# Hymba-style layer on one core: the order of the last norm, weight sums held back before the first keys, and weight sums made during the attention scores

## The chip, the cores and the metric

The kernel runs on one core of one Trainium2 chip. The metric is the device time of one execution in microseconds (us), the median of three runs. The core's engines are TensorE (PE in the profile, with PEld for its weight loads), VectorE (DVE), ScalarE (ACT), GpSimd (POOL) and SyncE (SP); each works off its own queue of instructions in the order in which they were written. Transfers are issued from SyncE's queue, and a few from ScalarE's.

## The reference

One layer over 512 tokens of width 2048, all in float32:

```python
def reference(x, mem, ...):
    h = x
    xn = _rmsnorm(h, norm_mix[l])
    y = xn @ w_in[l]
    o_gdn = _gdn_group(y[..., :GDN_COLS], ...)      # gated DeltaNet, 8 heads x 128
    o_rwkv = _rwkv_group(y[..., GDN_COLS:], ...)    # RWKV-7, 16 heads x 64
    h = h + jnp.concatenate([o_gdn, o_rwkv], axis=-1) @ w_out[l]
    h = h + _cross_attention(_rmsnorm(h, norm_xattn[l]), _rmsnorm(mem, norm_mem[l]),
                             wq, wk, wv, wo)        # 4 heads of 512, 256 memory tokens
    hn = _rmsnorm(h, norm_mlp[l])
    h = h + jnp.square(jax.nn.relu(hn @ mlp_w_up[l])) @ mlp_w_down[l]   # hidden 8192
    return _rmsnorm(h, norm_final)
```

`_rmsnorm(x, g)` is `x * rsqrt(mean(x*x) + 1e-6) * g`.

## The kernel before, in words

**Products.** Every float32 operand of a large product is cut into two float32r halves: ScalarE casts the high half (`whi`), VectorE subtracts it from the raw value for the low half (`wlo`), and TensorE adds hi·hi, hi·lo and lo·hi. A weight tile is 128x1024 (512 KB), loaded by SyncE into one of a few raw buffers (`wraw`, `w`, `ws`); each tile of halves has three buffers in the attention stages.

**Stages**, by the trace's time: the input projection (`py`, 0 to 907 us) with the chains of the two recurrent groups woven in; the keys of the memory tokens (`kp`, weights `in_wk`; the memory itself is loaded as `in_memT` into `wraw` and `mraw` and cut into `mhl`), from 907; the product of keys and query weights (`kq`), from 1025; values (`vp`, `vo`), from 1118; the output projection (`op`), from 1295; the scores (`sc`), 1456 to 1546; attention times values (`at`), to 1640; the MLP up (to 2280) and down (to 2874), which use Strassen's products; and the final norm with the outputs, to 2890.

**What sets the order.** In the scores and some other stages the program's text is the order, apart from the transfers, which a scheduler places by their buffers. In most other stages a planner does it: chains of Python generators yield instructions or conditions (`after(...)`, a lambda on `events`), and `run()` issues next the instruction with the earliest estimated start, plus 150 ns times the chain's rank for engines other than TensorE. All its instructions carry the line of the helper that records them, L257.

**Weight sums.** Strassen's products of the MLP down need the sums s1 to s4 of the quarters A11, A21, A22, A12 of the weight `w_dm`. For 13 pairs (e, m) of 2048 columns they are made ahead: `presum` loads a piece of the four quarters (tiles `ds`, or later `ab`, `sl`, `acc`, `h`), VectorE makes the four sums in place, and SyncE stores them to DRAM (`sd_s`), to be loaded later like a weight. `presums` does so in the projection and key stages in pieces of 410 columns with one set of `ds` buffers (40 pieces, 32 of 410 and 8 of 408 columns); `remaining` and `leftover` make the rest in the MLP.

**First keys.** In the recurrent part, `ndri`, `sr` and `bg16T`, `bg16U` are small transfers that carry a triangular inverse between engines: VectorE's `GA` and `GB` are written to `ndri`, then copied to `sr`, worked on by GpSimd, and written out as `bg16T` and `bg16U`. They stand on SyncE's queue in a row with the loads of the second `in_memT` tile, of the `in_wk` tiles and of `mraw`.

**Scores.** Two heads at a time (`g`), eight iterations each. An iteration loads a tile of 128x1024 in two halves (`kqr`, from DRAM `kqd`; three buffers), cuts it (`kqh`, `kql`), and runs 24 matmuls.

**The last norm.** When the MLP's last product for a token group t (128 tokens, t = 0 to 3) and column group g (512 columns) is added, `final` squares the tile on ScalarE with a running sum, and multiplies it by the gain for g = 0 and 1; when all four of a t are done, `store` forms the row's factor (reduce, square root, reciprocal), scales the four tiles (g = 0, 1 on ScalarE, g = 2, 3 on VectorE together with the gain) and writes each out (256 KB). T4 is the last of the last unit's products; t = 2, 3 finish first, then 0 and 1.

Of the kernel before, what the change touches and what calls it, by code (L numbers as in the profile page):

```python
# [17 lines left out]
P = 128  # L18
# [55 lines left out]
def build(tc, I, out):  # L74
# [53 lines left out]
    def split(src, hi, lo, gain=None):  # L128
        if gain is None:
            S.copy(hi, src)  # L130
            V.tensor_tensor(out=lo, in0=src, in1=hi.bitcast(F32), op=ALU.subtract)  # L131
        else:
            S.activation(hi, src, AF.Copy, scale=gain)
            V.scalar_tensor_tensor(out=lo, in0=src, scalar=gain, in1=hi.bitcast(F32),
                                   op0=ALU.mult, op1=ALU.subtract)
# [264 lines left out]
    def presum(e, m, c, n, d, LD=Lane(nc.sync, "SP", margin=5000.0), ST=SY):  # L400
        tt = lambda o, a, b, op=ALU.subtract: DV.tensor_tensor(out=o, in0=a, in1=b, op=op)
        src = I["w_dm"][e, m]
        a11, a21, a22, a12 = b = [x[:, 0:n - c] for x in d]
        for i in (A21, A22, A11, A12):
            yield LD.dma_start(b[i], src[i][:, c:n])
        for j, op in (("s1", tt(a22, a21, a22, ALU.add)), ("s3", tt(a21, a11, a21)),
                      ("s2", tt(a11, a22, a11)), ("s4", tt(a12, a12, a11))):
            yield op
            yield ST.dma_start(Sd[e, m, j][:, c:n], op[5])
            upto[e, m, j] = upto.get((e, m, j), 0) + n - c  # L410

    def presums(d, width, stop):
        while todo and not stop():
            e, m = todo.pop(0)
            for c in range(0, 2048, width):
                if c and stop():
                    todo.insert(0, (e, m))
                    return
                yield from presum(e, m, c, min(c + width, 2048), d, Lane(nc.sync, "SP", margin=5000.0), Lane(nc.sync, "SP", 0.0, 0.0))

    hk = [("w", I["wk"][n][:, h * 1024:(h + 1) * 1024]) for n, h in kpo]
# [1261 lines left out]
    def turned():  # L1683
        g, _, probs = turn.pop(0)
        for e in range(2):
            for mt in range(2):
# [4 lines left out]
                S.copy(phi[kk], pt)  # L1691
                V.tensor_tensor(out=plo[kk], in0=pt, in1=phi[kk].bitcast(F32), op=ALU.subtract)

    for g in range(2):
        banks = (("mm", 2), ("mg", 2), ("mg", 2), ("mm", 2)), (("scr", 1), ("scg", 1), ("mx", 2), ("mx", 2))
        pts = [psb(f"sc{g}_{t}", *banks[g][t]) for t in range(4)]
        for n2 in range(8):
            cnt[0] += 1
            raw = pw.tile([P, 1024], F32, tag="wraw", name=f"kqr{cnt[0]}", bufs=NWR)
            for i in range(2):  # L1700
                nc.sync.dma_start(raw[:, i * 512:(i + 1) * 512], KQd[2 * n2 + i][:, g * 512:(g + 1) * 512])
            wh = pw.tile([P, 1024], F32R, tag="whi", name=f"kqh{cnt[0]}", bufs=NWS)
            wl = pw.tile([P, 1024], F32R, tag="wlo", name=f"kql{cnt[0]}", bufs=NWS)
            split(raw, wh, wl)
            if g == 0 and n2 < 6:
                second(2 * n2 + 4)
                second(2 * n2 + 5)
            its = [(i, t) for i in range(2) for t in range(4)] if n2 < 7 else [(i, t) for t in range(4) for i in range(2)]
            for i, t in its:
                n = 2 * n2 + i  # L1710
                w1, w2 = wh[:, i * 512:(i + 1) * 512], wl[:, i * 512:(i + 1) * 512]
                a1, a2 = hh_[n][:, t * P:(t + 1) * P], hl_[n][:, t * P:(t + 1) * P]
                mm(pts[t], a1, w1, start=(n == 0), stop=False)
                mm(pts[t], a1, w2, start=False, stop=False)
                mm(pts[t], a2, w1, start=False, stop=(n == 15))
            if g == 0 and n2 == 6:
                norm()
            if g == 1 and n2 < 2:
                softmax(2 * n2)
                softmax(2 * n2 + 1)  # L1720
            if g == 1 and n2 == 3:
                turned()
        if g == 1:
            for n in range(2):
                begun.append((psb(f"at{n}", "mg"), *wload(VOd[0][:, :, n * P:(n + 1) * P])))
                attend(*begun[n], 0)
        turn.append((g, pts, []))
        if g == 1:
            for t in range(4):
                softmax(t)  # L1730
# [202 lines left out]
    def splits():  # L1933
        for u in units:
            if u[0] == "d" and u[1:3] in INSITU and u[1:] not in PRE:
                for i, w in order_of(u):
                    for x in xs(u):
                        yield (after("sum", u, w, x) if isinstance(w, str) else after("raw", u, w, x))
                        r = raws[u, {"s2": A11, "s3": A21, "s4": A11 if u == units[-1] else A12}.get(w, w), x]
                        halves[u, i, x] = hl = yield from take(hfree)  # L1940
                        yield from cut(r, *hl)
                        events.add(("half", u, i, x))
                        if w not in (A11, "s2") and (w != A12 or u == units[-1]):
                            wfree.append(r)
                continue
            if u[0] == "d":
                for i, w in order_of(u):
                    for x in xs(u):
                        yield after("raw", u, i, x)
                        halves[u, i, x] = hl = yield from take(hfree)  # L1950
                        yield from cut(raws[u, i, x], *hl)
                        wfree.append(raws[u, i, x])
                        events.add(("half", u, i, x))
                continue
            for i, w in order_of(u):
                yield ready((u, w))
                halves[u, i] = hl = yield from take(hfree)
                yield from cut(sums[u, w] if isinstance(w, str) else raws[u, w], *hl)
                events.add(("cut", u, w))
                events.add(("half", u, i))  # L1960
                if w in ("s1", "s2"):
                    release(u, w, sfree)
                elif w == "s3":
                    release(u, A21)
                elif w == "s4":
                    wfree.append(raws[u, A12])
                elif w != A12:
                    release(u, w)
# [204 lines left out]
    def downout(u, t, tag):  # L2173
        e, g = u[1:3]
        yield after("H", 3, 3)

        def add(m, half, src):
            h = H[2 * half + t, 2 * g + m]
            return tt(h, h, src)

        (x, kx) = banks_of[u, tag, t]
        mul = lambda i: after("mul", u, i, t)
        outs = {B11: (tag, 0, 0, 0), B21: ("mm", 0, 0, 1), T2: (tag, 0, 1, 0), T1: ("mg", 1, 1, 0),
                T3: (tag, 1, 1, 0), B22: ("mg", 0, 1, 1), T4: (tag, 1, 0, 1)}
        for i, _ in order_of(u):
            tg, m, half, end = outs[i]
            yield mul(i)
            b, kb = banks_of[u, tg, t]
            yield add(m, half, b)
            events.add(("snap", u, i, t))  # L2190
            if end:
                events.add(kb)
            if e == 3 and u[3:] != (0,) and i in (B21, T3, B22, T4):
                chain(final(2 * half + t, 2 * g + m), 0 if g and i == T4 else 2 if g == 0 else 1)
# [77 lines left out]
    def final(t, g):  # L2272
        h = H[t, g]
        c = yield from take(cfree)
        yield AC.activation(c, h, AF.Square, accum_out=cols5[t][:, g:g + 1])
        cfree.append(c)
        if g not in (2, 3):
            yield after("wf")
            yield tt(h, h, wf[g], ALU.mult)
        got[t] += 1  # L2280
        if got[t] == 4:
            chain(store(t), 1 if t > 1 else 0.2)

    def store(t):
        a, b = rows5[t][:, 0:1], rows5[t][:, 1:2]
        yield DV.tensor_reduce(out=a, in_=cols5[t], axis=AX.X, op=ALU.add)
        yield AC.activation(b, a, AF.Sqrt, scale=1.0 / 2048)
        yield DV.reciprocal(out=b, in_=b)
        yield after("wf")
        for g in (0, 1, 2, 3):  # L2290
            h = H[t, g]
            if g in (2, 3):
                yield DV.scalar_tensor_tensor(out=h, in0=h, scalar=b, in1=wf[g], op0=ALU.mult, op1=ALU.mult)
            else:
                yield AC.activation(h, h, AF.Copy, scale=b)
            yield (SV if g < 2 else SY).dma_start(out[t * P:t * P + P, g * 512:g * 512 + 512], h)

    def phase():
        return sum(("mul", v, B11, 0) in events for v in units[32:])
# [166 lines left out]
```

## Time and profile before

| | us |
|---|---|
| runs | 2887.84, 2888.71, 2888.92 |
| median of the runs | 2888.71 |
| the profiled execution, span from first to last instruction | 2890.0 |
| TensorE busy | 2862.2 (99%) |
| VectorE, ScalarE, GpSimd busy | 2333.9, 1571.7, 214.7 |
| moved by the DMA engines | 553 MB, 191 GB/s in the mean |

The profiled execution's span, 2890.0 us, is its own time; it stands 1.3 us above the median of the runs. The granted clock of TensorE was 0.999 of full speed in the mean. A duration read below is one of that execution. In rows of the trace the first number is the start in us from the span's begin, the second the duration; brackets give the engine's idle time ahead of the instruction and what ended it.

### The profile page before, as it was taken

To read this page: it belongs to the slowest core of one execution; us is meant where nothing else is said; L and a number is where in the kernel's file an instruction comes from. 1 tells how busy PE (TensorE), PEld (TensorE's weight loads), DVE (VectorE), ACT (ScalarE), POOL (GpSimd) and SP (SyncE) were. 2 spreads that over 40 slices of the span, in tenths; PEclk is the share of its full clock that TensorE was granted. 3 is DMA by queue.
4 is the path that set the end of the run, shared out by engine and by line. 5 is a ranking of instruction groups with operands and counts; after the bars stand their busy time and mean duration, and the time that the engine had idled before them with its cause. 6 is when DMAs were issued, how large, how long until landed. Compare 5 with 4: busy or idle time off the path is not lost.

```text
span 2890.0 us, 49168 instructions
## 1 busy us (share of the span) xinstructions
PE 2862.2 (99%) x18794; PEld 2419.1 (84%) x18794; DVE 2333.9 (81%) x3559; ACT 1571.7 (54%) x2233; POOL 214.7 (7%) x539
## 2 busy tenths in 40 slices
PE   9999999999999999999999999999999999999998
PEld 7877887877877888889988888888888888888887
DVE  7787787787877877769956898899998878786888
ACT  6555555645656655664445556555555644454544
POOL 0213213213212100000000000000000000000000
PEclk9999999999999999999999999999999999999999
DMA  5656656657656788784422354666565878887733
GB/s 191 166 147 176 176 149 187 165 154 189 180 161 200 214 257 274 232 292 151 124 95 88 110 164 153 199 195 207 189 200 178 292 249 277 295 257 247 265 101 110
DMA packets 321212, 553.01 MB, mean 191 GB/s; under 512 B 101128, under 2 KB 188428, under 8 KB 320976
## 3 DMA queue, kind: packets, MB, share of 16 engines
q1 hardware_dynamic: 293584, 518.41, 58.7%
q10 hardware_dynamic: 27392, 31.46, 3.1%
q8 instruction: 147, 2.41, 0.3%
q14 instruction: 89, 0.73, 0.1%
HBM read 443.45 MB, written 106.31 MB: 190 GB/s over the span
## 4 chain that ended last, share of the span: by engine, by line
PE 94%; DMA 3%; DVE 1%; ACT 1%; issue 1%; ACTq 0%; SPq 0%; DVEq 0%
PE py L257 22%; PE mxu L257 12%; PE mgd L257 6%; PE mgu L257 6%; PE mxd L257 6%; PE op L122 6%; PE vp L122 3%; PE mmu L257 3%; PE sc L122 3%; PE at L122 3%; PE scrd L257 3%; PE scgd L257 3%; PE mmd L257 3%; PE kq L257 3%; PE kp L257 2%; DMA wraw<-in_wo 1%
## 5 line engine op out<-in xcount | busy, mean ns | idle before, releaser
L257 ACT CAST whi<-wraw 128x1024 fp32r<-128x1024 f32 (+1 forms) x365 | 382.8, 1049 | 370.1 <-PE py L257 138.7
L257 DVE TENSOR_TENSOR wlo<-wraw,whi 128x1024 fp32r<-128x1024 f32 (+1 forms) x365 | 446.8, 1224 | 90.0 <-ACT whi L257 82.5
L257 PE MATMUL py<-xhi,whi 128*128 128x512 f32 x928 | 373.9, 403 | 6.8 <-ACT xhi L257 6.8
L257 PE MATMUL py<-xhi,wlo 128*128 128x512 f32 x928 | 373.1, 402 | 0.0
L257 PE MATMUL py<-xlo,whi 128*128 128x512 f32 x928 | 372.4, 401 | 0.0
L257 ACT CAST whi<-w 128x1024 fp32r<-128x1024 f32 x178 | 187.6, 1054 | 174.0 <-PE scgd L257 42.3
L257 DVE TENSOR_TENSOR wlo<-w,whi 128x1024 fp32r<-128x1024 f32 x178 | 217.3, 1221 | 43.4 <-ACT whi L257 40.9
L257 PE MATMUL mxu<-cb,whi 128*128 128x512 f32 x1016 | 249.3, 392 | 0.0
L257 PEld LDWEIGHTS mxu<-cb,whi 128*128 128x128 f32 x1016 | 184.7, 189 | 34.3
L257 PEld LDWEIGHTS py<-xhi,whi 128*128 128x128 f32 x928 | 175.3, 189 | 42.0 <-ACT xhi L257 6.8
L257 PEld LDWEIGHTS py<-xhi,wlo 128*128 128x128 f32 x928 | 175.3, 189 | 34.7 <-issue 1.0
L257 PEld LDWEIGHTS py<-xlo,whi 128*128 128x128 f32 x928 | 175.3, 189 | 33.8 <-DVE xlo L257 0.5
L131 DVE TENSOR_TENSOR wlo<-wraw,whi 128x1024 fp32r<-128x1024 f32 x112 | 136.7, 1222 | 44.8 <-ACT whi L130 44.3
L130 ACT CAST whi<-wraw 128x1024 fp32r<-128x1024 f32 x112 | 117.6, 1051 | 86.8 <-PE op L122 26.2
L257 PE MATMUL mxu<-cb,wlo 128*128 128x256 f32 x1016 | 142.7, 283 | 0.7 <-DVE wlo L257 0.7
L257 PEld LDWEIGHTS mxu<-cb,wlo 128*128 128x128 f32 x1016 | 135.1, 191 | 6.0 <-DVE wlo L257 0.9
L257 PE MATMUL mgu<-cb,whi 128*128 128x512 f32 x512 | 129.3, 394 | 0.1
L257 PE MATMUL mxd<-whi,cb 128*128 128x512 f32 x512 | 126.8, 389 | 0.0
L257 PE MATMUL mgd<-whi,cb 128*128 128x512 f32 x512 | 126.4, 389 | 0.0
L257 ACT ACT_TABLE_LOAD x87 | 111.6, 1283 | 16.5 <-DVE suml_gon L257 8.6
L122 PE MATMUL op<-ob,whi 128*128 128x256 f32 (+1 forms) x752 | 115.2, 304 | 0.0
L257 ACT CAST whi<-ws 128x1024 fp32r<-128x1024 f32 x75 | 79.0, 1053 | 64.0 <-PE mgu L257 48.1
(943 smaller groups left out, 6429.3 us busy)
## 6 DMA issues: line engine op xcount, KB each, us to landing
wraw<-in_w_in SPq DMA_DIRECT2D x116, 512.0 KB, 4.7
wraw<-in_w_up SPq DMA_DIRECT2D x65, 512.0 KB, 3.6
w<-in_w_up SPq DMA_DIRECT2D x63, 512.0 KB, 4.2
ds<-in_w_dm SPq DMA_DIRECT2D x128, 205.0 KB, 4.4
sd_s<-ds SPq DMA_DIRECT2D x128, 205.0 KB, 4.9
wraw<-sd_s SPq DMA_DIRECT2D x51, 512.0 KB, 4.9
w<-sd_s SPq DMA_DIRECT2D x50, 512.0 KB, 5.5
w<-in_w_dm SPq DMA_DIRECT2D x48, 512.0 KB, 4.9
```

The source lines that it names most:

```text
L122: PE.matmul(o, l, r, start=start, stop=stop, skip_group_check=again)
L130: S.copy(hi, src)
L131: V.tensor_tensor(out=lo, in0=src, in1=hi.bitcast(F32), op=ALU.subtract)
L257: f(*a, **k)
```

## The change

Four edits go together.

1. In `presums` a condition stands ahead of each piece: after ("py", 55) and before ("kp", 1) no new piece is begun. 38 pieces are made there instead of 40.
2. In the scores, 15 further pieces of 256 columns (one of 50) are made: `fetched` loads the four quarters on SyncE (L1702), `summed` makes the sums on VectorE behind the next iteration's cut (L1709), `stored` writes them out (L1717); the buffers are `ds0` to `ds3`, two of each. The MLP makes correspondingly less: of pieces of 512 columns in `sl` and `acc` there are 2 instead of 7.
3. After the cut of sum s1 of certain units, the planner waits until s2 is planned.
4. In the last norm the chains' ranks, the order of the groups and some waits of the planner change; 15 of the 16 outputs are issued by SyncE and one by ScalarE, instead of eight by each.

```diff
 def presums(d, width, stop):
...
+                yield lambda: ("py", 55) not in events or ("kp", 1) in events
                 yield from presum(e, m, c, min(c + width, 2048), d, Lane(nc.sync, "SP", margin=5000.0), Lane(nc.sync, "SP", 0.0, 0.0))
...
+    spans = [(e, m, c, min(c + M, 2048)) for e, m in todo for c in range(upto.get((e, m, "s4"), 0), 2048, M)]
+    held, made_ = [], []
+
+    def fetched(s):
+        e, m, c, n = spans.pop(0)
+        b = [pl.tile([P, M], F32, tag=f"ds{i}", name=f"ds{s}_{i}", bufs=2)[:, 0:n - c] for i in range(4)]
+        for i in (A21, A22, A11, A12):
+            nc.sync.dma_start(b[i], I["w_dm"][e, m][i][:, c:n])
+        held.append((e, m, c, n, b))
+
+    def summed():
+        e, m, c, n, (a11, a21, a22, a12) = held.pop(0)
+        for j, o, x, y, op in (("s1", a22, a21, a22, ALU.add), ("s3", a21, a11, a21, ALU.subtract),
+                               ("s2", a11, a22, a11, ALU.subtract), ("s4", a12, a12, a11, ALU.subtract)):
+            V.tensor_tensor(out=o, in0=x, in1=y, op=op)
+            made_.append((Sd[e, m, j][:, c:n], o))
+            upto[e, m, j] = n
+        if n == 2048:
+            todo.remove((e, m))
+
+    def stored():
+        while made_:
+            nc.sync.dma_start(*made_.pop(0))
+
     for g in range(2):
...
             wl = pw.tile([P, 1024], F32R, tag="wlo", name=f"kql{cnt[0]}", bufs=NWS)
+            stored()
+            if g * 8 + n2 < 15:
+                fetched(g * 8 + n2)
             split(raw, wh, wl)
+            if g * 8 + n2:
+                summed()
...
                 attend(*begun[n], 0)
+            stored()
...
                         events.add(("half", u, i, x))
+                        if w == "s1":
+                            yield after("sum", u, "s2", x)
...
             yield mul(i)
             b, kb = banks_of[u, tg, t]
+            if u == units[-1] and i == T4:
+                yield after("gained", t, 1)
+                yield after(*(("scaled", 0, 1) if t else ("scaled", 3, 1)))
             yield add(m, half, b)
...
             yield after("wf")
+            if (t, g) == (1, 1):
+                yield after("snap", units[-1], T4, 0)
             yield tt(h, h, wf[g], ALU.mult)
+            events.add(("gained", t, g))
         got[t] += 1
         if got[t] == 4:
-            chain(store(t), 1 if t > 1 else 0.2)
+            chain(store(t), 0.05)
 
     def store(t):
...
         yield DV.reciprocal(out=b, in_=b)
+        chain(scaled(t, b), {2: 0.4, 3: 0.5, 0: 0.6, 1: 0.05}[t])
+
+    def scaled(t, b):
         yield after("wf")
-        for g in (0, 1, 2, 3):
+        for g in (2, 0, 1, 3) if t == 0 else (2, 0, 3, 1):
+            if (t, g) == (0, 3):
+                yield after("snap", units[-1], T4, 1)
             h = H[t, g]
...
-            yield (SV if g < 2 else SY).dma_start(out[t * P:t * P + P, g * 512:g * 512 + 512], h)
+            yield (SV if (t, g) == (1, 1) else SY).dma_start(out[t * P:t * P + P, g * 512:g * 512 + 512], h)
+            events.add(("scaled", t, g))
```

The rows below are one engine's instructions in the order in which its queue holds them. First SyncE's queue about 30 us before the first keys; `in_wk` and `in_memT` are weight and memory loads of `kp`. Before:

```order
L257 DMA ds_54_828<-in_w_dm 128x410
L257 DMA ds_55_829<-in_w_dm 128x410
L257 DMA ds_53_827<-in_w_dm 128x410
L257 DMA ndri_10094<-GA_10025 64x8x64
L257 DMA ndri_10094<-GB_10026 64x8x64
L257 DMA ds_56_830<-in_w_dm 128x410
L257 DMA sr_10099<-ndri_10094 64x16x16
L257 DMA wraw_10126<-in_wk 128x1024
L257 DMA wraw_10175<-in_memT 128x1024
L257 DMA sd_1_s_154<-ds_55_829 128x410
L257 DMA mixd_90<-gkt_10013 128x512
L257 DMA sd_1_s_156<-ds_54_828 128x410
```

and with the change:

```order
L257 DMA sd_0_s_153<-ds_56_830 128x408
L257 DMA ndri_10091<-GA_10025 64x8x64
L257 DMA ndri_10091<-GB_10026 64x8x64
L257 DMA sr_10096<-ndri_10091 64x16x16
L257 DMA wraw_10122<-in_wk 128x1024
L257 DMA wraw_10171<-in_memT 128x1024
L257 DMA mixd_90<-gkt_10013 128x512
L257 DMA gqd_10197<-Rd 128x512
L257 DMA lg_10315<-in_g2a 128x128
```

The loads of one piece of sums and the stores of its results no longer stand between and behind the small transfers.

Next, SyncE's queue in the scores; `kqd` is the DRAM tile that an iteration loads in two halves. Before:

```order
L1701 DMA kqr_16623<-kqd_110 128x512
L1701 DMA kqr_16623<-kqd_111 128x512
L1701 DMA kqr_16662<-kqd_112 128x512
L1701 DMA kqr_16662<-kqd_113 128x512
L1701 DMA kqr_16702<-kqd_114 128x512
L1701 DMA kqr_16702<-kqd_115 128x512
```

and with the change:

```order
L1702 DMA ds_0_17141<-in_w_dm 128x256
L1702 DMA ds_3_17144<-in_w_dm 128x256
L1726 DMA kqr_17179<-kqd_113 128x512
L1717 DMA sd_1_s_162<-ds_2_17096 128x256
L1717 DMA sd_1_s_164<-ds_1_17095 128x256
L1717 DMA sd_1_s_163<-ds_0_17094 128x256
L1717 DMA sd_1_s_165<-ds_3_17097 128x256
L1726 DMA kqr_17226<-kqd_114 128x512
L1702 DMA ds_1_17189<-in_w_dm 128x256
L1702 DMA ds_2_17190<-in_w_dm 128x256
L1702 DMA ds_0_17188<-in_w_dm 128x256
L1702 DMA ds_3_17191<-in_w_dm 128x256
L1726 DMA kqr_17226<-kqd_115 128x512
```

The two halves of a `kqr` tile now stand apart, with the stores of one piece of sums (`sd`) ahead of the first half and the loads of another between the halves.

Last, VectorE's queue at the end of the program. `r` is a token group's row factor (r_17962 before and r_18178 after is that of t = 0, r_17963 and r_18179 that of t = 1, r_17965 and r_18181 that of t = 3); the additions of `mxd` are the last product's, for t = 0 and then t = 1. Before:

```order
L257 TENSOR_TENSOR h_12823<-h_12823,mxd_1_0_0_27238 128x512
L257 TENSOR_REDUCE r_17962<-c_17958 128x1
L257 TENSOR_TENSOR h_12819<-h_12819,h_12825 128x512
L257 SCALAR_TENSOR_TENSOR h_12822<-h_12822,r_17965,sl_17955 128x512
L257 RECIPROCAL r_17962<-r_17962 128x1
L257 SCALAR_TENSOR_TENSOR h_12824<-h_12824,r_17965,sl_17956 128x512
L257 TENSOR_TENSOR h_12823<-h_12823,mxd_1_0_1_27239 128x512
L257 SCALAR_TENSOR_TENSOR h_12821<-h_12821,r_17962,sl_17955 128x512
L257 TENSOR_REDUCE r_17963<-c_17959 128x1
L257 SCALAR_TENSOR_TENSOR h_12823<-h_12823,r_17962,sl_17956 128x512
L257 RECIPROCAL r_17963<-r_17963 128x1
L257 SCALAR_TENSOR_TENSOR h_12821<-h_12821,r_17963,sl_17955 128x512
```

and with the change:

```order
L257 SCALAR_TENSOR_TENSOR h_12798<-h_12798,r_18181,sl_18171 128x512
L257 TENSOR_TENSOR h_12795<-h_12795,h_12801 128x512
L257 SCALAR_TENSOR_TENSOR h_12800<-h_12800,r_18181,sl_18172 128x512
L257 TENSOR_TENSOR h_12799<-h_12799,mxd_1_0_0_27394 128x512
L257 TENSOR_TENSOR h_12795<-h_12795,h_12801 128x512
L257 TENSOR_REDUCE r_18178<-c_18174 128x1
L257 RECIPROCAL r_18178<-r_18178 128x1
L257 SCALAR_TENSOR_TENSOR h_12797<-h_12797,r_18178,sl_18171 128x512
L257 TENSOR_TENSOR h_12799<-h_12799,mxd_1_0_1_27395 128x512
L257 SCALAR_TENSOR_TENSOR h_12799<-h_12799,r_18178,sl_18172 128x512
L257 TENSOR_REDUCE r_18179<-c_18175 128x1
L257 RECIPROCAL r_18179<-r_18179 128x1
```

The second addition of `mxd` has moved from behind two scalings of t = 3 (r_17965) with the reciprocal between them, to behind one scaling of t = 0; the scalings of t = 3 stand before the first addition now.

## The prediction

> **What bounds the kernel now.** I read the head of the page first, then TensorE's waits, then the stretches by stage.
>
> ```profile
> span 2890.0 us, 49168 instructions
> PE 2862.2 (99%) x18794; PEld 2419.1 (84%) x18794; DVE 2333.9 (81%) x3559; ACT 1571.7 (54%) x2233; POOL 214.7 (7%) x539
> ```
>
> TensorE is busy for 2862.2 of 2890.0 us, and the change adds and removes no matmul; a gain can only come out of the other 27.8 us. Where those lie, the waits and the stretches say (in a stretch: its length, then the busy time of TensorE, its weight loads, VectorE, ScalarE and GpSimd, the granted clock, the DMA share and GB/s):
>
> ```profile
> PE py L257 <- ACT xhi L257: 6.8, 1, 6.8
> PE kp L257 <- DVE wlo L257: 2.7, 1, 2.7
> PE rs L257 <- DVE Qs L257: 2.2, 2, 1.2
> PE gs L257 <- DVE TtG L257: 1.2, 1, 1.2
> PE kq L257 <- DVE y L257: 1.1, 1, 1.1
> ```
>
> ```profile
> 1456.00:1546.00 90.00, 90.00 (x410) 74.71 (x409) 38.01 (x62) 32.85 (x57) 0.00 (x0) 1.00 0.31 97
> ...
> 2280.00:2874.00 594.00, 594.00 (x2622) 491.84 (x2621) 487.18 (x580) 294.45 (x349) 0.00 (x0) 1.00 0.70 232
> 2874.00:2890.00 16.00, 5.83 (x26) 4.50 (x24) 9.03 (x18) 7.58 (x17) 0.00 (x0) 0.80 0.71 247
> ```
>
> The 6.8 us are the start and untouched. The tail holds 16.00 − 5.83 = 10.17 us and the first key weights 2.7 us; these two the change can shorten. The scores and the down projection have no idle time at all: there the change can only lose.
>
> **Part 1, sums held back before the first keys.** The chain behind the 2.7 us, in order of time, and SyncE's queue (start, duration):
>
> ```profile
> 899.80 7.03 DMA mraw<-in_memT
> ...
> 906.92 0.52 ACT mhl L257
> ...
> 907.70 5.51 DMA wraw<-in_wk
> ...
> 913.29 1.05 ACT whi L257
> ```
>
> ```profile
> 873.10 1.47 SPq L257 DMA_DIRECT2D ds<-in_w_dm  x3
> 874.62 0.60 SPq L257 DMA_DIRECT2D ndri<-GA  x1
> ...
> 876.00 0.67 SPq L257 DMA_DIRECT2D ds<-in_w_dm  x1
> 878.44 0.59 SPq L257 DMA_DIRECT2D sr<-ndri  x1
> ...
> 883.30 0.33 SPq L257 DMA_DIRECT2D sd_s<-ds  x1
> ...
> 896.32 0.58 SPq L257 DMA_DIRECT2D bg16T<-sr  x1
> ```
>
> ```profile
> 899.00:914.00 15.00, 13.94 (x69) 11.64 (x68) 7.62 (x16) 9.47 (x18) 0.00 (x0) 1.00 1.03 276
> ```
>
> The key weight that ends the wait is issued at 907.70 (the start of its row in the chain) and lands after 5.51 us, with the DMA engines full (1.03) from 899 to 914. Held back are the piece whose loads stand at 873.10 and 876.00, its four stores, and one further piece. The three loads ahead of `ndri` take 1.47 us of the queue; without them `ndri`, then `sr` (878.44), then the GpSimd work up to `bg16T` (896.32) come up to that much earlier, and so the transfers behind it, until the key weight waits for its turn among them. I take 1.5 us off the 2.7. Bounds: 0 if the full engines, not the queue, set the landing (two raw key and memory loads ahead of it wait for ScalarE's and TensorE's buffers, which don't move); 2.7 if the stores that fell beside 908 slowed the landing too. Nothing in the rows makes this wait longer. The held pieces resume behind the seventh key weight: four loads of 205 KB, which by 276 GB/s hold the engines for 0.84 MB / 276 = 3.0 us once, at a place where three raw buffers lie ahead; 0, with a loss of at most those 3.0 us. The transposes moved inside `kp` stay the same matmuls; the 1.2 us of `gs` and of `rs` may go or double; 0.
>
> **Part 2, sums in the scores.** Added there: 60 loads, 60 sums, 60 stores; elsewhere 28 fewer of each, 20 of these in the down projection, where TensorE was busy in 594.00 of 594.00 us: no gain from that. The added VectorE work:
>
> ```profile
> L257 DVE TENSOR_TENSOR h<-h x24: 415/416/427, 1843.6 to 2348.6; 128x256 f32<-128x256 f32 x24
> ```
>
> ```profile
> 1467.51 1.22 DVE L131 TENSOR_TENSOR kql<-kqr,kqh 128x1024 fp32r<-128x1024 f32 x1 [2.83 <-ACT kqh L130]
> 1472.95 1.23 DVE L131 TENSOR_TENSOR kql<-kqr,kqh 128x1024 fp32r<-128x1024 f32 x1 [4.22 <-ACT kqh L130]
> ```
>
> ```profile
> 1471.87 1.05 ACT L130 CAST kqh<-kqr 128x1024 fp32r<-128x1024 f32 x1 [4.39 <-PE sc L122]
> ```
>
> ```profile
> 1466.00:1476.00 10.00, 10.00 (x46) 8.29 (x45) 2.45 (x2) 2.11 (x2) 0.00 (x0) 1.00 0.25 83
> ```
>
> An iteration takes 1472.95 − 1467.51 = 5.44 us. VectorE idles 4.2 us of it; four sums of 0.42 are 1.7 us and fit. A half `kql` is finished at 1472.95 + 1.23 = 1474.18, 2.3 us after TensorE gave its buffer free (1471.87). Three buffers make it due two iterations after that: 10.88 − 2.3 = 8.6 us of slack. Cover for VectorE: this slack.
>
> The queue is the narrow place. `kqr` now stands between stores and loads of sums, and each set of loads waits until the stores from its buffers (two sets) have landed:
>
> ```profile
> sd_s<-ds SPq DMA_DIRECT2D x32, 204.0 KB, 2.8
> ...
> h<-in_w_dm SPq DMA_DIRECT2D x24, 128.0 KB, 3.3
> sd_s<-h SPq DMA_DIRECT2D x24, 128.0 KB, 4.9
> ```
>
> One turn of the queue is the second store's issue (0.34, as the 0.33 of the row at 883.30), its landing L, four loads (1.36) and half a `kqr` (0.34): 2.04 + L. It keeps up with TensorE's 5.44 for L up to 3.4. The rows bound L by 2.8 (stores of 204 KB in lighter traffic) and 4.9 (stores of this size beside the heavy traffic of the MLP). An iteration would move 8 x 128 KB and 512 KB = 1.57 MB, which is 289 GB/s against 83 now and 373 at best (below): busy, not full. I take L near 3, nearer to 2.8: cost 0. At 4.9 a turn is 6.94, 1.5 late, over 11 turns 16.5, less the 8.6 of slack: 8 us lost. A loss starts at L = 3.4 + 8.6 / 11 = 4.2.
>
> **Part 3, the added wait on sum s2** moves no row on any engine's order: 0.
>
> **Part 4, the last norm.** VectorE, ScalarE, and the stretches at the end:
>
> ```profile
> 2880.03 0.73 DVE L257 SCALAR_TENSOR_TENSOR h<-h,r,sl 128x512 f32<-128x512 f32 x1
> 2880.68 0.68 DVE L257 TENSOR_TENSOR h<-h,mxd 128x512 f32<-128x512 f32 x1
> ...
> 2882.66 0.16 DVE L257 TENSOR_REDUCE r<-c 128x1 f32<-128x5 f32 x1 [0.64 <-ACT acc L257]
> ```
>
> ```profile
> 2881.29 0.72 ACT L257 ACTIVATE h<-h,r 128x512 f32<-128x512 f32 x1 [0.42 <-ACT rstd L257]
> 2881.92 0.61 ACT L257 ACTIVATE acc<-h 128x512 f32<-128x512 f32 x1
> ...
> 2885.50 0.34 ACTq L257 DMA_DIRECT2D out_dram<-h  x1
> ```
>
> ```profile
> 2879.00:2881.00 2.00, 0.83 (x4) 0.37 (x2) 2.00 (x5) 0.74 (x2) 0.00 (x0) 1.00 0.56 176
> 2881.00:2884.00 3.00, 0.00 (x0) 0.00 (x0) 2.33 (x6) 1.95 (x5) 0.00 (x0) 0.94 1.02 354
> 2884.00:2888.00 4.00, 0.00 (x0) 0.00 (x0) 1.00 (x2) 1.03 (x2) 0.00 (x0) 0.50 1.01 373
> 2888.00:2889.00 1.00, 0.00 (x0) 0.00 (x0) 0.00 (x0) 0.00 (x0) 0.00 (x0) 0.50 0.09 29
> ```
>
> TensorE ends at 2879.83. The last addition (`h<-h,mxd`, group t=1) then waits behind a scaling until 2880.68; in the new order those scalings (of t=3) are done before TensorE ends, so it starts near 2879.95, 0.73 earlier. ScalarE's square behind it started 1.24 late (2881.92 for an addition that began at 2880.68), behind a scaling of t=0 at 2881.29. The two scalings of t=0 still stand ahead of it, but no output is issued between them (0.34) and no scaling of t=3 delays VectorE's reciprocal that releases them, so I put the square at 2880.65, when the addition is done. The reduction falls from 2882.66 to 2881.4 and the last issue from 2885.50 to about 2883.4: 2.1 us. But the transfers bound the end: 3 x 354 + 4 x 373 = 2.55 MB in the saturated 7 us, 9.7 outputs of 256 KB, 0.72 us each. Now t=2 and t=3 are out of the way earlier, in the idle 0.44 of 2879–2881, so that the eight outputs of t=0 and t=1 drain from about 2880.95 (t=0 issued from 2879.95, by my estimate up to 1 us to the first byte) in 8 x 0.72 = 5.8 us: last byte at 2886.7, against 2888.1. Gain 1.4; bounds 0 (the eight start no earlier in sum) and 2.1 (the issue alone sets it). SyncE's queue issues 15 outputs at 0.34; it idles between them, and ScalarE saves seven issues of 0.34 to 0.37.
>
> "DMAs initiated by the scalar, sync or gpsimd engine will ultimately run on the same 16 DMA engines and interleave with each other" is the Trainium skill, page "DMA: Bandwidth & Descriptors", section "Issuing engines are not separate DMA queues". The 1.01 at 373 GB/s with both queues in use agrees; by that rule moving seven outputs to SyncE speeds up no transfer, and the gain here is from the earlier additions alone. By the same page's fit in "Anatomy of one DMA" (bytes / 436 GB/s behind some 2 us fixed) an output would take an estimated 0.60 us, eight 4.8, and the tail's gain would be 2.4; the measured 0.72 decides.
>
> **Sum.** −1.5 − 1.4 ± 0 = −2.9 on the profiled 2890.0, thus 2887.1; that execution is 1.3 above the median of the runs, 2888.71, so 2885.8. A change under 0.2% (5.8 us) is hard to tell from none in this kernel.
>
> **The rivals.** A, slower: the queue in the scores falls behind, by the sum above from L = 4.2; at L = 4.9 8 us, less the 2.9: 2893.8. For it speaks the 4.9 row and 289 GB/s; against it the 2.8 row and 8.6 us of slack. Past 2894.5 it would need L over 5.
>
> B, it does nothing: the landing from 899 to 914 is set by full DMA engines, and the tail's drain by 16 outputs of 0.72; the waits keep their 2.7 and 10.2. For it speak 1.03 and 1.01; against it that less is moved ahead of both. 2888.2, between 2887.3 and 2890.
>
> C, everything named closes: 2.7 + 2.1 and the waits of `gs`, `rs` and `kq` (1.2 + 1.2 + 1.1) = 8.3: 2880.4. Against it: those three hang on the VectorE chains of `kp` and `kq`, into which the held sums are pushed.
>
> **How the numbers follow.** Forecast 0.60 (2883.5 to 2888), B 0.15, A 0.15, C 0.10. Faster by over 0.2% is most of C: 0.08. Slower by over 0.2% needs 2894.5 or L near 5, plus what the resumed sums in `kp` might cost: 0.09. The rest, 0.83, is within. The range 2882.9 to 2890.5 leaves out C and the larger part of A, 0.2 together, and holds the bounds 2.7 + 2.1 with one of the 1.2.
>
> **What would show it.** TensorE's wait of `kp` on `wlo` near 1.2 us instead of 2.7 and the key weight issued near 906.2; no wait of `sc` on `kql`, stores of sums in the scores landing in about 3 us, and VectorE near 4.2 us of 10 there; the down projection's TensorE still full; the tail 8.8 us behind TensorE's end, the last output issued near 2883.4 less what was gained before. A wait of `sc`, or of a `kp` matmul beyond the first, would make it wrong.

## The result, and the profile after

The changed kernel is slower: 2903.68 us in the median of five runs (2902.71 to 2911.73) against 2888.92 (2887.84 to 2889.93), a ratio of 1.0054 with a 95% interval of 1.0042 to 1.0066 (the ratios below have theirs in brackets). The forecast was 2885.8 with a range of 2882.9 to 2890.5. The profiled execution spans 2901.6 us and took 2903.41.

TensorE's waits after, as they were read before:

```profile
PE ptr L1690 <- DVE plo L1693: 9.5, 1, 9.5
PE py L257 <- ACT xhi L257: 7.8, 1, 7.8
PE kp L257 <- DVE wlo L257: 2.6, 1, 2.6
PE pvt L257 <- DVE gv L257: 2.0, 1, 2.0
...
PE sc L122 <- DVE kql L131: 0.8, 1, 0.8
...
PE sc L122 <- ACT kqh L130: 0.7, 1, 0.7
```

The first line is new and the largest: in the scores TensorE waits 9.5 us for `plo`, the low half of the transposed probabilities. The stretches (columns as in the prediction) say the same of the stage:

```profile
1456.00:1546.00 90.00, 79.11 (x353) 65.03 (x352) 53.98 (x109) 28.40 (x46) 0.00 (x0) 0.94 0.75 232
...
2280.00:2874.00 594.00, 594.00 (x2628) 492.12 (x2628) 474.68 (x558) 296.95 (x351) 0.00 (x0) 1.00 0.65 221
```

Where the time went is best read from when the first matmul of each stage starts. A group's row gives the first and the last start. Before, then after:

```profile
L122 PE MATMUL sc<-kqh,hh x128: 388/389/486, 1455.3 to 1544.5; 128*128 128x512 f32 x128
...
L122 PE MATMUL at<-phi,whi x128: 387/389/497, 1545.2 to 1634.1; 128*128 128x512 f32 x128
...
L257 PE MATMUL mgd<-whi,cb x512: 389/389/389, 2303.0 to 2862.2; 128*128 128x512 f32 x171
```

```profile
L122 PE MATMUL sc<-kqh,hh x128: 389/389/775, 1455.2 to 1557.5; 128*128 128x512 f32 x128
...
L122 PE MATMUL at<-phi,whi x128: 387/389/497, 1558.2 to 1647.0; 128*128 128x512 f32 x128
...
L257 PE MATMUL mgd<-whi,cb x512: 389/389/389, 2316.0 to 2875.2; 128*128 128x512 f32 x171
```

Up to the scores nothing changed (1455.3, 1455.2). The scores take 1558.2 − 1455.2 = 103.0 us instead of 89.9: 13.1 lost. From there to the first `mgd` product of the MLP down all is shifted by 13.0. From that product to the end it is 2901.6 − 2316.0 = 585.6 us instead of 587.0: 1.4 gained. 13.1 − 1.4 − 0.1 is the 11.6 by which the spans differ.

**What happens in the scores.** ScalarE's casts of `kqh`, which had come every 5.44 us, one per iteration:

```profile
1466.31 1.05 ACT L130 CAST kqh<-kqr 128x1024 fp32r<-128x1024 f32 x1 [2.54 <-issue]
...
1474.21 1.05 ACT L130 CAST kqh<-kqr 128x1024 fp32r<-128x1024 f32 x1 [6.22 <-DMA kqr<-kqd]
1482.39 1.05 ACT L130 CAST kqh<-kqr 128x1024 fp32r<-128x1024 f32 x1 [7.13 <-DMA sd_s<-ds]
1489.02 1.05 ACT L130 CAST kqh<-kqr 128x1024 fp32r<-128x1024 f32 x1 [5.58 <-DMA sd_s<-ds]
...
1534.90 1.05 ACT L130 CAST kqh<-kqr 128x1024 fp32r<-128x1024 f32 x1 [4.51 <-DMA sd_s<-ds]
```

They wait on transfers instead of on TensorE. The two turns from 1466.31 to 1482.39 take 16.1 us, 5.2 more than TensorE's 10.9; the eight to 1534.90 take 52.5, 9.0 more than 43.5. The lateness at the end is 14.2. In the first two turns the queue issues almost without a break (27 issues in the 15.0 us from 1465.58 to 1480.62) and then stands 2.4 us for a store that takes 4.4 to land. SyncE's queue in one of the later turns:

```profile
1485.80 1.95 SPq L1717 DMA_DIRECT2D sd_s<-ds  x4
1487.84 0.38 SPq L1726 DMA_DIRECT2D kqr<-kqd  x1
1489.72 1.76 SPq L1702 DMA_DIRECT2D ds<-in_w_dm  x4
1491.52 0.43 SPq L1726 DMA_DIRECT2D kqr<-kqd  x1
1492.00 2.18 SPq L1717 DMA_DIRECT2D sd_s<-ds  x4
```

and the chain that ended last, through the same turn:

```profile
1486.28 3.38 DMA sd_s<-ds
...
1491.52 0.43 SPq L1726
...
1492.00 0.43 SPq L1717
...
1492.47 3.42 DMA sd_s<-ds
```

From one store's landing to the next: 6.2 us. The queue issues for 4.5 of them, and stands from 1488.22 to 1489.72 until the store behind which the next load's buffer comes free has landed.

TensorE has a lead of two iterations over the casts. By the twelfth cast, at 1515.72, it is used up: TensorE waits 0.7 us for that `kqh` and 0.8 us for its `kql`. These 1.4 us (1.44 before rounding) are what the late cuts cost directly up to there. The large wait comes from the order behind them. On ScalarE the first `phi`, the high half of the transposed probabilities, stands behind the cast for a later iteration, and on VectorE `plo` stands behind the cut and the sums of a later one:

```profile
1528.37 1.04 ACT L130 CAST kqh<-kqr 128x1024 fp32r<-128x1024 f32 x1 [5.40 <-DMA sd_s<-ds]
1529.33 1.07 ACT L1692 CAST phi<-ptr 128x512 fp32r<-128x512 f32 x2
```

```profile
1529.45 1.22 DVE L131 TENSOR_TENSOR kql<-kqr,kqh 128x1024 fp32r<-128x1024 f32 x1 [1.70 <-ACT kqh L130]
1531.98 1.34 DVE L1709 TENSOR_TENSOR ds<-ds,ds 128x256 f32<-128x256 f32 x3 [1.30 <-DMA ds<-in_w_dm]
1534.22 0.42 DVE L1709 TENSOR_TENSOR ds<-ds,ds 128x256 f32<-128x256 f32 x1 [0.90 <-DMA sd_s<-ds]
1534.56 1.28 DVE L1693 TENSOR_TENSOR plo<-ptr,phi 128x512 fp32r<-128x512 f32 x2
```

```profile
1525.45 0.39 PE L122 MATMUL sc<-kqh,hl 128*128 128x512 f32 x1
1535.30 1.97 PE L1690 MATMUL ptr<-cst,pr 128*128 128x128 f32 x8 [9.46 <-DVE plo L1693]
1536.92 0.78 PE L122 MATMUL sc<-kqh,hh 128*128 128x512 f32 x1
```

The third of four groups of transposes needs the bank (a part of TensorE's result memory) that the first `plo` frees. So TensorE waits until ScalarE and VectorE have worked through a cut that it needs only 18 products later, and VectorE through sums that it does not need in this stage at all. In this one wait the lead is built up again: the cast at 1542.05 waits for TensorE as before.

The wait has a second price. The first product behind it took 0.78 us instead of 0.39, and the granted clock was 0.50 in the trace from 1535 to 1538 and 1.00 from 1539 on. The 16 transposes and the 96 products from 1523.43 to the end of the stage take 25.3 us without the wait, against 23.6 for the same work in the kernel before: about 1.7 of the 13.1 us.

### The profile page after: what moved, and what is told of

Its sections match the earlier page's. It is cut to its first block, busy times and chain, and to the rows that moved or that the text cites. A ratio compares the mean times of both kernels' runs of the same rounds, so it can differ in the third digit from the quotient of the medians.

```text
span 2901.6 us, 49344 instructions
## 1 busy us (share of the span) xinstructions
PE 2865.0 (99%) x18794; PEld 2422.3 (83%) x18794; DVE 2336.2 (81%) x3591; ACT 1571.9 (54%) x2233; POOL 216.3 (7%) x539
## 4 chain that ended last, share of the span: by engine, by line
PE 93%; DMA 3%; DVE 2%; SPq 1%; ACT 1%; issue 0%; DVEq 0%; ACTq 0%
PE py L257 22%; PE mxu L257 12%; PE mgd L257 6%; PE mgu L257 6%; PE mxd L257 6%; PE op L122 5%; PE vp L122 3%; PE mmu L257 3%; PE at L122 3%; PE vo L122 3%; PE scrd L257 3%; PE scgd L257 3%; PE mmd L257 3%; PE kp L257 3%; PE kq L257 3%; DMA sd_s<-ds 2%
```

## The experiments

Two theories stand against each other on the loss in the scores. Theory 1: SyncE's queue, which cannot turn in 5.44 us, sets all of it. Theory 2: the queue's lateness less TensorE's lead would be 4 to 6 us, and the rest is the order in which `plo` stands. Times are compared with runs of the kernel before on the same chip, whose median was 2892.42, 2891.52, 2893.65 and 2891.18 us in the four sets, above the 2888.92 of the first. Each set ran on a chip of its own, so times are compared within a set. A stage's length is read from one profiled execution, as above. In the scores such readings are steady: all seven kernels that make no sums there, or sums in every second iteration only, show 89.9 us. Ahead of the scores they are not: from the first key product to the first score product the kernel before and the one with the sums in the scores alone have the same code, and show 548.1 and 552.7 us.

**Without the sums in the scores.**

```diff
-            stored()
-            if g * 8 + n2 < 15:
-                fetched(g * 8 + n2)
             split(raw, wh, wl)
-            if g * 8 + n2:
-                summed()
```

> The changed kernel without the sums in the scores (they are made in the MLP again); the other three edits stay. Theory 1, the whole loss is made in the scores: TensorE is full there again (90.0 of 90 us from 1456 to 1546) and the time is 1.0 to 2.9 us under the kernel before, about 2886.5 (tail 1.4 shorter, the stretch up to the scores about 1.2 shorter). Rival, held-back sums or the new tail cost too: 2888.9 or more.

Measured: 2891.31 us, ratio 1.0000 (0.9991 to 1.0010); the scores take 89.9 us (1455.9 to 1545.8). The loss comes from the sums in the scores. The rest of the change gains nothing that the runs can tell.

**The sums in the scores alone**, put into the kernel before.

> The kernel before with the sums in the scores alone. Theory 1: 13 us more from the first score product to the first of the attention times values (103 us against 89.9), the time about 13 us over the kernel before. Rival, the loss needs the held-back sums too (they leave more columns for the scores or shift the stages): under 8 us.

Measured: 2903.70 us, ratio 1.0046 (1.0031 to 1.0061); 100.7 us in the scores, a wait of 8.5 on `plo`. Part 2 needs no help from the others; the stage loses 10.8 us instead of the expected 13, and the time 12.2.

**Four banks for the transposes**, with VectorE's, ScalarE's and SyncE's orders the same row by row:

```diff
-            pt = psb(f"ptr{g}_{e}_{mt}", "mm", 2)
+            pt = psb(f"ptr{g}_{e}_{mt}", "mg" if g == 0 and e else "mm", 2)
```

> The changed kernel with four PSUM banks instead of two for the four transposes of the probabilities inside the scores; the orders of VectorE, ScalarE and SyncE are the same. Theory 2, the queue's lateness of 0.8 us a turn alone would leave 13 - 8.6 = 4 to 6 us; the rest comes from TensorE waiting at the third transpose for a bank that VectorE frees (plo) only behind a cut and sums that run two iterations ahead: the loss falls by 6 to 9 us, to 2895 to 2898. Theory 1 alone, the late queue sets the whole loss whatever TensorE waits on: 2902 to 2905.

Measured: 2896.77 us, ratio 1.0018 (1.0008 to 1.0027), so 4.4 us over the kernel before instead of some 14.8. The scores take 93.6 us. The waits of this kernel:

```profile
PE sc L122 <- DVE kql L131: 1.7, 3, 0.8
...
PE ptr L1690 <- DVE pr L1681: 0.8, 1, 0.8
...
PE sc L122 <- ACT kqh L130: 0.7, 1, 0.7
...
PE ptr L1690 <- DVE plo L1693: 0.5, 1, 0.5
```

The 9.5 us are gone with nothing changed on the queue, whose stores still land in 3.4 us; TensorE makes all 16 transposes in one row. The two `ptr` lines lie in the stage after the scores, which is 1.6 us longer here (1547.5 to 1638.7, against 89.6 us), so that 5.3 us of loss stay together. Theory 2 holds: about 5 of the 13.1 us are the late data themselves, and some 8 are the wait for `plo` with the slower matmuls behind it, a wait that the late queue makes long. A kernel with `plo` ahead of the cut and the sums on VectorE was not run.

**Three buffers against two.** Both kernels have pieces of 208 columns and differ in the buffers alone.

```diff
-    spans = [(e, m, c, min(c + M, 2048)) ... range(..., 2048, M)]
+    spans = [(e, m, c, min(c + 208, 2048)) ... range(..., 2048, 208)]
...
-        b = [pl.tile([P, M], ..., bufs=2)...]
+        b = [pl.tile([P, 208], ..., bufs=3)...]      # the control: bufs=2
```

> The changed kernel with pieces of 208 columns instead of 256 in the scores and three buffers for each quarter instead of two. Theory 1, a turn of SyncE's queue in the scores is ten issues of 0.47 us plus the wait for a store that has just been issued to land (3.4 us), 6.2 to 6.5 us against TensorE's 5.44: without that wait a turn is ten issues, 4.7 us, and the loss is gone: 2886 to 2888. Rival, the DMA engines are too busy for it (share 0.75 to 0.86): with 0.81 of the bytes some loss stays, 2892 to 2900, as with two buffers.

> The control for three buffers: 208 columns, two buffers. Theory 1: the same number of issues and the same wait for the landing, which is hardly shorter (3.2 for 3.4): turns of about 6.0 us, loss of 9 to 13 us against three buffers: 2896 to 2901. Rival, bytes decide: the loss shrinks with them to the same as with three buffers, 2886 to 2892.

Measured: with three buffers 2894.62 us, ratio 1.0005 (0.9996 to 1.0015), scores 92.2 us; with two 2900.18, ratio 1.0030 (1.0016 to 1.0044), scores 98.4. The same bytes and issues, and 6.2 us apart: the wait for the store just issued carries 6.2 of the 8.5 us that two buffers lose at this width. With three, ten issues stand close:

```profile
1518.73 1.92 SPq L1717 DMA_DIRECT2D sd_s<-ds  x4
1520.70 2.75 SPq L1702 DMA_DIRECT2D ds<-in_w_dm  x4
1523.54 0.85 SPq L1726 DMA_DIRECT2D kqr<-kqd  x2
1524.49 1.95 SPq L1717 DMA_DIRECT2D sd_s<-ds  x4
```

A turn is still 5.8 here, not the expected 4.7; 2.3 us of the loss stay, 2.0 of them in waits of `ptr` on `plo`. The expectation of no loss was missed. Whether the rest is the busier engines (stores landed in 3.8 us here) or VectorE's order stays open.

**One load for the four quarters.**

```diff
-        for i in (A21, A22, A11, A12):
-            nc.sync.dma_start(b[i], I["w_dm"][e, m][i][:, c:n])
+        nc.sync.dma_start(t[:, :, 0:n - c], I["w_dm"][e, m].rearrange("i p c -> p i c")[:, :, c:n])
```

> The changed kernel with the four loads of a piece in the scores joined into one transfer of 512 KB (one tile, one issue): seven issues on SyncE's queue per turn instead of ten, the same bytes. Theory 1, first form, the number of issues decides: a turn is 1.4 us shorter, under 5.44, and the scores take 90 to 92 us instead of 103. Theory 1, second form, the wait for a store just issued decides: the one load now waits for all four stores of its buffer, 1.0 us later than before, so a turn is 1.9 + 3.4 + 0.5 + 0.5 = 6.3 us and the scores still take 99 us or more.

Measured once: 2909.42 us; the scores take 103.4, the wait for `plo` is 11.5. With seven issues the queue still turns in 6.2 us (nine turns between the loads at 1486.06 and 1541.44), as the second form said: fewer issues do not help where the load waits for the last store of its buffer. But this run does not split the loss as cleanly as the pair above, because the orders on the other engines moved too. ScalarE's casts come every 5.44 us, waiting for TensorE, up to 1499.35; the lateness begins only when VectorE has the softmax, and later `plo`, behind sums that wait for their transfers (4.0 us ahead of the sum at 1540.43, behind which `plo` stands).

**A piece in every second iteration.**

```diff
-            if g * 8 + n2 < 15:
+            if n2 % 2 == 0:
                 fetched(g * 8 + n2)
             split(raw, wh, wl)
-            if g * 8 + n2:
+            if n2 % 2:
                 summed()
```

> The changed kernel with one piece of 256 columns in every second iteration of the scores (8 pieces instead of 15), the rest of the sums in the MLP as before. Theory 1: a turn of some 6.3 us has 10.88 us of TensorE's work to hide behind, so that the scores take 90 us again and the time is 0 to 2 us under the kernel before. Rival, any sum there is in TensorE's way through VectorE's queue (plo behind sums): the scores stay 3 to 6 us longer.

Measured: 2892.07 us, ratio 1.0004 (0.9995 to 1.0013); scores 89.9 us (1457.7 to 1547.6). Half of the sums cost nothing there, though `plo` and the sums share VectorE's queue as before. The time is not seen to be under that of the kernel before, though the interval reaches to 1.4 us under it; the keys' stage, taken up next, is longer here.

**The new last norm alone.**

> The kernel before with the new order of the last norm and its outputs alone. The prediction's step: 1.4 us less from TensorE's last products to the end (26.4 us from the last unit's first mgd product with a high weight half, against 27.8), and no other stage moves: 1.4 us under the kernel before. Rival, outputs in one queue drain slower: same or slower.

Measured: 2891.56 us, ratio 0.9997 (0.9988 to 1.0006). From the first `mgd` product to the end 2888.4 − 2302.8 = 585.6 us, 1.4 less than before. All kernels with the new norm and no new wait in the MLP show 585.3 to 585.6, those without it 586.9 or 587.0. The gain stands in every profile and is too small for the runs' times to show.

**The sums held back alone.**

> The kernel before with part 1 alone (no new piece of sums between py 55 and kp 1). Prediction's step: the first key weight is ready 1.5 us earlier and the time falls by that. Rival, seen in the profile of the changed kernel: TensorE also arrives 1.3 us earlier at the first keys and then waits the same 2.6 us there, and a new wait of 2.0 us on gv (pvt) takes what is left: no change, within 1 us of the kernel before.

Measured: 2893.67 us, ratio 1.0008 (0.9999 to 1.0018). The keys to the first `kq` product take 118.5 us (910.0 to 1028.5), against 115.1 in the kernel before and in the one with the last norm alone; 2.8 are the new wait at `pvt`. All eight kernels that hold until kp 1 have this wait, of 1.4 to 3.1 us, and the five others have none over 0.4. The stage's length scatters more: 116.7 to 118.7 us in seven of the eight, but 113.3 in the one with four banks. The wait is seen in the changed kernel's profile. SyncE's queue before and after, and VectorE's after:

```profile
966.77 0.33 SPq L257 DMA_DIRECT2D sd_s<-ds  x1
967.14 0.42 SPq L257 DMA_DIRECT2D bg8T<-sgi  x1
...
974.88 7.44 SPq L257 DMA_DIRECT2D wraw<-in_wk  x4
```

```profile
966.39 1.49 SPq L257 DMA_DIRECT2D ds<-in_w_dm  x3
967.92 0.43 SPq L257 DMA_DIRECT2D bg8T<-sgi  x1
...
976.86 6.84 SPq L257 DMA_DIRECT2D wraw<-in_wk  x4
```

```profile
982.13 1.23 DVE L257 TENSOR_TENSOR wlo<-wraw,whi 128x1024 fp32r<-128x1024 f32 x1 [2.86 <-ACT whi L257]
983.27 0.69 DVE L257 SCALAR_TENSOR_TENSOR gv<-sg,gv 128x512 f32<-128x512 f32 x1
```

A resumed piece's loads stand ahead of `bg8T`; the key weight behind it is issued at 976.86 instead of 974.88, and `gv`, which `pvt` needs, stands behind the cut at 982.13, where it had stood ahead of the cut at 980.74 before.

**Held back longer, until kp 8**, without sums in the scores.

```diff
-                yield lambda: ("py", 55) not in events or ("kp", 1) in events
+                yield lambda: ("py", 55) not in events or ("kp", 8) in events
```

> The changed kernel without the sums in the scores, and with the sums held back until kp 8 instead of kp 1, so that no resumed piece's loads stand on SyncE's queue ahead of bg8T and the key weights behind it. Theory, these loads (1.9 us of the queue) delay the key weight behind which VectorE has the last gv product, and so make the new wait of 2.0 to 3.1 us at pvt: the weight is issued near 975 instead of 976.9 to 978.7 (if the keys start at 906 to 907), the wait falls under 1 us, the first keys to the first kq product take 115 to 116 us instead of 116.7 to 118.7, and the time is 1.5 to 3 us under the kernel before. Rival, the wait comes from VectorE's order alone (gv behind the cut): it stays at 2 us or more.

Measured: 2902.34 us, ratio 1.0033 (1.0021 to 1.0046). The keys take 112.9 us (908.3 to 1021.2), below the expected 115 to 116, with no wait at `pvt`; both the loads ahead of `bg8T` and VectorE's order changed, so which of them made the wait stays open. The time is not as expected, since the MLP now has a wait it never had:

```profile
PE scrd L257 <- ACT whi L257: 9.8, 1, 9.8
```

From `mgd`'s first product to the end it takes 600.0 us instead of 585.6. The chain behind the wait begins with a late sum: its store out of `sl` lands at 2736.48, the loads behind it on SyncE's queue start after that, and the load that the cast needs lands at 2744.69. This kernel makes 10 pieces in `sl` and `acc`, against 7 in the kernel before and 9 in the kernel without sums in the scores, which shows no such wait. What is not made early must still find its place in the MLP.

**Both together**: held back until kp 8, a piece in every second iteration of the scores, and the new last norm.

> What the runs so far point to: the sums held back until kp 8, one piece in every second iteration of the scores (8 pieces), the new last norm. Theory: before the scores 2 to 3.5 us are gained (no wait at pvt), the scores take 89.9 us, the MLP has 24 transfers of the late kind (sl and acc) against 28 in the kernel before and 40 in the one that was held to kp 8 without sums in the scores, and shows no new wait, the tail is 1.4 us shorter: 3.4 to 5 us under the kernel before. Rival, the MLP's wait at scrd of 9.8 us comes back, since the pieces are late whatever their number: 5 us or more over the kernel before.

Measured: 2887.21 us, ratio 0.9989 (0.9980 to 0.9998): 3.2 us by the ratio under the kernel before, just short of the expected 3.4 to 5. It is the only kernel here whose interval lies below 1, and by less than the 5.8 us at which the prediction drew the line. Keys 112.1 us, scores 89.9, no wait in the MLP of over 0.7, tail 1.4 shorter; the wait of `kp` on `wlo` was 1.1 us in this execution.

## Why the prediction was right or wrong

**Part 2, wrong, and it decides.** The mechanism was there as rival A with a chance of 0.15, and the form of the sum was right: one store's issue, its landing L, four loads and half a `kqr`. Two of its sizes were not. "2.04 + L" with L near 3 came to 6.2 us: an issue took 0.33 to 0.43 and 0.05 or more to the next, where the 0.34 came from single ones, so that the six issues took 2.8; and the landing took 3.4, above the 2.8 and well under the 4.2 from which the prediction saw a loss. The Trainium skill's page "DMA: Bandwidth & Descriptors", section "Issuing engines are not separate DMA queues", calls the time to initiate a DMA "usually small relative to the DMA itself". With ten issues in a turn of 6.2 us it was 4.5 us of queue here, while these transfers landed in 2.5 to 3.6 us in the median.

These sizes alone would not have shown the loss: by the prediction's own sum 0.8 us late over 11 turns, less 8.6, leaves next to nothing. The step that failed is that subtraction, "8.6 us of slack. Cover for VectorE: this slack". The prediction named TensorE's lead as the cover and did not ask what else stands on VectorE and ScalarE behind the leading work. `plo` and `phi` do, and through them TensorE waits for the lead to be rebuilt. So 14.2 us of lateness became 13.1 us of loss, where the subtraction would have left 5.6; with the four banks that untie `plo` it was 5.3. Of the 14.2, the first two turns made 5.2, and the prediction had no term for them.

**Part 1, its first step right, its value wrong.** The first key weight was issued 0.85 us earlier (906.85 instead of 907.70) and landed 0.55 faster, and its low half was ready for TensorE at 914.24 instead of 915.65: 1.4 us earlier, against 1.5 forecast. But TensorE arrived 1.3 us earlier too, and waited 2.6. The 2.7 us from which the 1.5 was taken are no steady quantity either: the three profiles without the hold show 2.7, 3.0 and 1.4 us at this place, and the eight that hold until kp 1 show 0.7 to 2.6. One profile could not carry a term of 1.5. The other step that failed is "four loads of 205 KB ... 0, with a loss of at most those 3.0 us": the resumed loads met the small transfers of the second recurrent group, and with them came the wait at `pvt` of 1.4 to 3.1 us.

**Part 3** moved nothing that is seen, as said: the kernel with the new norm alone lacks it and shows the same 585.6 us. **Part 4, right**, in the steps as in the sum: 1.4 us of gain forecast and 1.4 measured, in every kernel that has it and no new wait in the MLP. The last addition and the square behind it after:

```profile
2892.94 0.68 DVE L257 TENSOR_TENSOR h<-h,mxd 128x512 f32<-128x512 f32 x1
...
2893.72 0.63 ACT L257 ACTIVATE acc<-h 128x512 f32<-128x512 f32 x1
```

Less the 13.0 us of shift these are 2879.9 and 2880.7, where the prediction has 2879.95 and 2880.65; the last issue, at 2896.80, came 0.4 later than forecast. The term of up to 1 us to the first byte stands in no row of its own. The outputs after:

```profile
2894.00:2897.00 3.00, 0.00 (x0) 0.00 (x0) 2.02 (x5) 1.98 (x5) 0.00 (x0) 1.00 1.04 350
2897.00:2899.00 2.00, 0.00 (x0) 0.00 (x0) 0.00 (x0) 0.00 (x0) 0.00 (x0) 0.50 1.03 385
2899.00:2900.00 1.00, 0.00 (x0) 0.00 (x0) 0.00 (x0) 0.00 (x0) 0.00 (x0) 0.50 0.62 236
```

The transfers run at 350 to 385 GB/s, with the engines full from 2894 to 2899, and the last byte leaves near 2899.6 (the 0.62 of the last row), which is 2886.6 less the shift, against 2886.7 forecast. That fits an end set by the transfers rather than by the last issue; no run separates the two. By the fit in the section "Anatomy of one DMA" of the Trainium skill's page "DMA: Bandwidth & Descriptors", which the page gives for transfers issued by GpSimd, the gain was estimated at 2.4; these outputs are issued by SyncE and ScalarE, and the trace shows 1.4.

**The sum** was −2.9 for all but the scores; the kernel without the sums there measured a ratio of 1.0000 (0.9991 to 1.0010), which just reaches down to −2.6. Part 1's gain is what was missing, as far as one can tell within that interval.

## What to carry to other kernels

Where loads go into buffers that have just been stored from, on one queue in order, the queue stands for a whole landing in every turn: count issues at their cadence, add the landing, and compare with the loop's time before counting on idle engines. A lead is slack only if nothing that the consumer needs sooner stands in the producer's queue behind the leading work; look for it by name. Work that is held back must be traced to where it resumes and to where the last of it ends up: the hold until kp 1 brought a wait at `pvt`, and the hold until kp 8 without sums in the scores a longer one in the MLP. And a wait that one profile shows should be looked up in a second one before a gain is taken off it.

## What the runs showed that was not expected

An issue on SyncE's queue took 0.42 to 0.54 us from one to the next in the turn shown, though single ones elsewhere show 0.33. The late queue cost more through an order on other engines than through its own lateness, and behind the long wait the granted clock was 0.50 for some 3 us. And the MLP's room for late sums may have a sharp edge: with 9 pieces in `sl` and `acc` no wait was seen, with 10 one of 9.8 us. Whether the number alone makes it is not shown, since the kernel with 10 also places other pieces differently.
